# Two streams for the block inverses, and VectorE steps pinned to the written order

## The chip, the cores and the metric

The kernel runs on one core of a Trainium2 chip. The time is device microseconds of one execution; lower is better. The core has five engines that run side by side, each working through its own queue in order: TensorE (PE in the profile; PEld is its weight load), VectorE (DVE), ScalarE (ACT), GpSimd (POOL), and SyncE (SP), which issues the DMAs here. An engine waits for another one only where the program makes it wait on a semaphore.

## The reference

One layer of a streaming encoder, for 64 sample tokens and 512 prompt tokens in float32, so 576 rows of width 1024:

```
h   = RMSNorm(x);  p = h @ w_in                       # r, k, v, three low-rank inputs, u, v_gmlp, gate_A, gate_B
o_A = RWKV-7 over p:  S = S * w_t + (S a_t) b_t^T + v_t k_t^T;  y_t = S r_t      # per head, 16 heads of 64
o_B = u * (tril(W_s) LayerNorm(v_gmlp) + b)
m   = sigmoid(gate_A) * (o_A @ w_proj_a) + sigmoid(gate_B) * (o_B @ w_proj_b)
x   = x + RMSNorm(m @ w_o);  x = x + RMSNorm(SwiGLU(RMSNorm(x)))
```

The recurrence for S is what the change touches. The kernel does not run it token by token. It cuts the tokens in chunks of 64 (9 chunks: one of the sample group, eight of the prompt), and within a chunk the rank-one updates of 64 tokens become one product with the inverse of a unit triangular 64 x 64 matrix. Between chunks only a short chain is left: the state of a chunk times a 128 x 128 matrix, plus a constant part.

## The kernel before

**Products.** All large products split each float32 operand into a high part (`whi`, made on ScalarE) and a rest (`wlo`, made on GpSimd, line 305, two halves of 512 columns for each weight block), and run three matmuls for each one. Weights come in blocks of 512 KB (`raw`).

**Pairs.** The 16 heads are worked off as 8 pairs. For each pair p there are these streams, each a Python generator:

- `elementwise(p)`: decays and normalised vectors from the projected r, k, v; among the rest a scan on VectorE (`L`, line 670) and the four scalings `AR` and `BK` (lines 719 to 722); then the chunk matrices `AB` and `AK` (matmuls named `am`). It writes the 16 x 16 diagonal blocks of `AB` to DRAM (`d_inv`, eight DMAs, line 750). It signals "A" once the second lot of `am` matmuls (32 of them) is issued and "elem" at its end.
- `turns(p)`: transposes, signals "tb" and "values".
- `inverse(p)`: the inverse of each 64 x 64 triangle. First the substitution: the 80 diagonal blocks of 16 x 16 are read from DRAM with one block on a partition (`M`, line 855), and 15 steps on VectorE follow, each a product into `Xt` (line 863) and an addition into `X` (line 866). Then the result goes back through DRAM into `IV` (one DMA out, line 868, eight in, line 872), and two levels of merging follow: VectorE transposes `IV` to `IT` (`turn()`, line 875), small matmuls `m`, `m`, and again `turn()`, matmuls `mp`, `mu`. It signals "it".
- `batch(p)`: from `IT`, matmuls `d`, then `e` and `c`, which VectorE turns into the chain matrices `TD` and the `AR` half (lines 966 and 967); signals "d", "inv", and after matmuls `y` "wide".
- `chain(p)`: seven steps; each is a matmul `pc` (two in the first step) and a sum on VectorE, `dst = pc + C` (line 1005; the destination is `S`, or `So` for the two final states). The next `pc` reads that sum. Signals "chain".
- `finish(p)`: group norm and gate, stores o_A ("oa").

**The order of the work.** The order of TensorE is written by a planner, the class `Weave`. It holds a clock, `now`, that each matmul moves on by an estimate. A stream yields the wait until its next piece (a number out of the table `LAT`, in microseconds, or an event with a number to add), and `run` issues whichever stream is due, the first in the list of streams before the others. When none is due it issues a slice of a large product (`pj`, the projections; later `gv`): three or six matmuls. So the numbers in `LAT` are no waits of the chip; they say how much other work the planner puts between two pieces of a stream.

TensorE keeps that order exactly (`manual_schedule`). On the other engines, the DMA queue of SP among them, the framework re-sorts the instructions by its own estimate of when each is ready. `tc.keep_in_program_order(ins)` restrains that: the instruction stays behind the one that was traced just before it on its engine. Before the change only the first product of a substitution and some others, `turn()` among them, are pinned so; the later substitution steps and the chain's sums are free to be moved.

`inv_all()` runs the inverses of the eight pairs one after the other: `inverse(p)` starts when "A" of pair p is signalled and `inverse(p - 1)` has ended. The streams stand in the list as `chain_all(), fin_all(), batch_all(), inv_all(), turn_all(), elem_all(), ...`.

Of the kernel before, what the change touches and what calls it, by code (L numbers as in the profile page):

```python
# [8 lines left out]
ALU = mybir.AluOpType  # L9
# [11 lines left out]
NPAIR = NH // 2  # L21
# [16 lines left out]
LAT = {  # L38
# [4 lines left out]

# [1 line left out]
}  # L45
# [15 lines left out]
SB = 16  # L61
NU = 2 * (64 // SB) * 10
# [171 lines left out]
def layer(tc, I, O):  # L234
# [35 lines left out]
    clk = Weave()  # L270
# [577 lines left out]
        clk.signal("values", hp_)  # L848


    def inverse(E):

        hp_, AB, di = E["hp"], E["AB"], d_inv[E["hp"]]
        M = rp.tile([P, SB, SB], F32, tag="M", name="M")[0:NU]
        sp.dma_start(M.rearrange("u s t -> u (s t)"), di[0].rearrange("h b u s t -> (h b u) (s t)"))
        X = rp.tile([P, SB, SB], F32, tag="X", name="X")[0:NU]
# [3 lines left out]
        for s in range(0, SB - 1):  # L860
            w, r = SB - 1 - s, s + 1
            t3 = tmp[:, 0:r * w].rearrange("u (j t) -> u j t", t=w)
            ins = dve.tensor_tensor(t3, X[:, 0:r, s:s + 1].broadcast_to([NU, r, w]), M[:, s:s + 1, s + 1:SB].broadcast_to([NU, r, w]), ALU.mult)  # L863
            if s == 0:
                tc.keep_in_program_order(ins)
            dve.tensor_tensor(X[:, 0:r, s + 1:SB], X[:, 0:r, s + 1:SB], t3, ALU.add)  # L866
            yield LAT["X"]
        sp.dma_start(di[1].rearrange("h b u s t -> (h b u) (s t)"), X.rearrange("p i t -> p (i t)"))
        for h in range(2):
            for b in range(64 // SB):  # L870
                r0_ = 64 * h + SB * b
                sp.dma_start(IV[r0_:r0_ + SB, :, SB * b:SB * b + SB], di[1, h, b].rearrange("u s t -> s u t"))
# [119 lines left out]
    def chain(E):  # L992


        AR, C, S0, hp_ = (E[n] for n in ("AR", "C", "S0", "hp"))
        add = lambda c: C[:, PLACE[c][1], PLACE[c][0], :]
        state = lambda c: S0 if c == 0 else add(1) if c == 2 else S[:, c, :]
        for n, cs in enumerate([(2, 0)] + [(c,) for c in range(3, NCH)]):
            pc = ps1c("pc").rearrange("p (i v) -> p i v", v=HD)
            for i, c in enumerate(cs):  # L1000
                mmul(pc[:, i], TD[:, c, :], state(c), start=True, stop=True)
            for i, c in enumerate(cs):
                last = c in (0, NCH - 1)
                dst = rp.tile([P, HD], F32, tag="So", bufs=2, name="So") if last else S[:, c + 1, :]
                dve.tensor_tensor(dst, pc[:, i], add(c), ALU.add)  # L1005
                if last:
                    sp.dma_start((O["wkv_s"] if c == 0 else O["wkv_p"])[hp_], dst)
            yield LAT["S"]

        yield (("wide", hp_), LAT["y"])  # L1010
        Y = E["Y"]
        yield from clk.free(2)
        py = [ps1("py", 2.2)[:, 0:320].rearrange("p (j v) -> p j v", v=HD) for _ in range(2)]
        for c, j, half_ in PLACES2:
            for h, rows in enumerate(HR):
                mmul(py[h][HR[half_], j], AR[rows, 1, c * 64:(c + 1) * 64], state(c)[rows], start=True, stop=True, skip_group_check=True)
        for h in range(2):
            dve.tensor_tensor(Y[:, :, HR[h]], py[h], Y[:, :, HR[h]], ALU.add)
        clk.signal("chain", hp_)
# [45 lines left out]
    def elem_all():  # L1065
# [13 lines left out]
        for i in range(2):  # L1079
            sp.dma_start(R["ln"][i][0:64], I["rows"][i:i + 1, :].broadcast_to([64, D]))  # L1080

    def inv_all():
        for p_ in range(NPAIR):
            yield (("A", p_), 0.0)
            yield from inverse(EV[p_])

    def turn_all():
        for p_ in range(NPAIR):
            yield (("A", p_), 0.0)
            yield from turns(EV[p_])  # L1090

    def batch_all():
        for p_ in range(NPAIR):
            yield from batch(EV[p_])

    def chain_all():
        for p_ in range(NPAIR):
            yield (("inv", p_), LAT["ch0"])
            yield from chain(EV[p_])

    def fin_all():
        for p_ in range(NPAIR):
            yield (("chain", p_), 0.0)
            yield from finish(EV[p_])
# [408 lines left out]
    with tc.manual_schedule(engines={mybir.EngineType.PE}):  # L1513
        lora = {0: lora_w(lora_raw(0), pin=False)}
        for nm, b in (("k", BLK_K), ("r", BLK_R), ("v", BLK_V)):
            take = Shifted(b, nm, scale=True)
            EV[0][nm] = [take(h, raw0[nm][:, HS[h]]) for h in range(2)][1]
            clk.signal(nm, 0)
        clk.run(chain_all(), fin_all(), batch_all(), inv_all(), turn_all(), elem_all(), norm1(0), norm1(1), norm2(0), norm2(1), hidden(), oa_all(), ob_all(),
                ln_all(), norm3(0), norm3(1))  # L1520
    R["o"].close()
    R["d0"].close()
# [19 lines left out]
```

## Time and profile before

| | |
|---|---|
| time, median of 3 runs | 1225.54 us (1216.94 to 1228.83) |
| the profiled execution | 1224.4 us, its span from the first to the last instruction 1222.6 us |
| PE busy | 1179.4 us of the span, 96% |
| DVE, ACT, POOL busy | 524.0, 466.9, 612.7 us |
| mean granted TensorE clock | 0.994 |
| pairs, about | 85 to 575 us of the span, some 58 us a pair |

A line of the timeline gives start, duration, engine, source line, operation, written tile and read tiles, shapes, count, and in brackets the idle time of the engine before it with what ended it. A line of the waits gives the waiting engine and tile, the releaser, the total in us, how often, and the longest. Since nearly every matmul is recorded by one helper (line 286), tile names tell the products apart. A line of the stretches gives, for each engine, busy us and the number of instructions; after them stand the granted clock as a share of full speed, the DMA share and GB/s.

### The profile page before, as it was taken

The numbers are of one execution on the slowest core, as the hardware profiler recorded it, in microseconds if no ns is written. First come the engines' busy times: TensorE is split into PE (matmuls) and PEld (weight loads), VectorE is DVE, ScalarE is ACT, GpSimd is POOL, SyncE is SP. The second block draws the span as 40 slices with busy tenths as digits, with TensorE's granted clock in tenths as the row PEclk, the third lists the DMA queues.
The fourth block names the chain that finished last, engine by engine and source line by source line (L and its number), as shares of the span: only waits on it lengthen the run. The fifth ranks groups of instructions, "written<-read, shape, count | busy, mean of one in ns | idle before, by whom it ended". The sixth has DMA issues, their size and how long they took to land.

```text
span 1222.6 us, 29930 instructions
## 1 busy us (share of the span) xinstructions
PE 1179.4 (96%) x12926; PEld 1145.2 (94%) x12926; DVE 524.0 (43%) x1081; ACT 466.9 (38%) x889; POOL 612.7 (50%) x484
## 2 busy tenths in 40 slices
PE   7999999999999999999899999899999999999997
PEld 6999889899998999999899999899999999999996
DVE  5756365656555655432615331753333333300003
ACT  5555534453545453342512333533222222222220
POOL 6675353546363535233645453566555655634442
PEclk9999999999999999999999999899999999999999
DMA  5243223132322222332644542332222222242222
GB/s 186 78 109 106 82 51 95 48 94 49 97 66 78 76 80 82 91 101 82 216 142 127 186 124 69 99 107 80 87 87 78 79 86 87 82 156 83 80 77 78
DMA packets 68276, 118.05 MB, mean 97 GB/s; under 512 B 30832, under 2 KB 36208, under 8 KB 68144
## 3 DMA queue, kind: packets, MB, share of 16 engines
q1 hardware_dynamic: 68000, 116.06, 31.5%
q8 instruction: 101, 1.65, 0.6%
q14 instruction: 31, 0.25, 0.1%
q10 hardware_dynamic: 144, 0.08, 0.0%
HBM read 99.83 MB, written 16.28 MB: 95 GB/s over the span
## 4 chain that ended last, share of the span: by engine, by line
PE 75%; DVE 14%; ACT 3%; DMA 3%; issue 3%; POOL 2%; SPq 0%; DVEq 0%; ACTq 0%; POOLq 0%
PE fg L286 21%; PE po L286 15%; PE pj L286 15%; PE pb L286 4%; PE pa L286 3%; PE gv L286 3%; DVE Xt L863 2%; DVE X L866 2%; PE am L286 1%; PE z L286 1%; PE m L286 1%; POOL wlo L305 1%; PE pc L286 1%; PE wv L286 1%; PE d L286 1%
## 5 line engine op out<-in xcount | busy, mean ns | idle before, releaser
L305 POOL TENSOR_TENSOR wlo<-raw,whi 128x512 fp32r<-128x512 f32 (+1 forms) x288 | 398.3, 1406 | 352.1 <-ACT whi L302 326.5
L302 ACT ACTIVATE whi<-raw 128x1024 fp32r<-128x1024 f32 x144 | 149.9, 1045 | 281.7 <-PE fg L286 174.6
L1293 DVE TENSOR_TENSOR rs<-rs,nsq 128x288 f32<-128x288 f32 (+2 forms) x12 | 9.0, 754 | 106.0 <-ACT nsq L1292 106.0
L1361 DVE TENSOR_TENSOR ft<-ft,fg 128x288 f32<-128x288 f32 x40 | 16.4, 451 | 68.2 <-PE fg L286 66.7
L1355 DVE TENSOR_TENSOR fg<-fg,rs 128x288 f32<-128x288 f32 x40 | 16.4, 453 | 63.3 <-PE fg L286 63.2
L1358 DVE SCALAR_TENSOR_TENSOR ft<-ft,fg 128x576 f32<-128x576 f32 (+1 forms) x24 | 28.8, 1200 | 18.7 <-ACT ft L1357 18.7
L1359 POOL TENSOR_TENSOR ft<-ft,rs 128x576 f32<-128x576 f32 (+1 forms) x24 | 31.8, 1324 | 7.1 <-DVE ft L1358 7.1
L688 POOL TENSOR_TENSOR aq<-aq,k 128x576 f32<-128x576 f32 x8 | 11.4, 1421 | 34.4 <-PE pc L286 30.0
L286 PE MATMUL pc<-S,TD 128*128 128x64 f32 x112 | 20.2, 262 | 8.6 <-DVE So L1005 8.6
L863 DVE TENSOR_TENSOR Xt<-X,M 80x15 f32<-80x15 f32 (+7 forms) x120 | 25.8, 215 | 4.8 <-DMA M<-d_inv 1.2
L286 PE MATMUL pj<-h5h,whi 128*128 128x288 f32 x88 | 27.8, 316 | 0.0
L286 PE MATMUL pj<-h1h,whi 128*128 128x288 f32 x88 | 27.8, 316 | 0.0
L286 PE MATMUL pj<-h0h,whi 128*128 128x288 f32 x88 | 27.8, 315 | 0.0
L286 PE MATMUL pj<-h2h,whi 128*128 128x288 f32 x88 | 27.7, 315 | 0.0
L286 PE MATMUL pj<-h6h,whi 128*128 128x288 f32 x88 | 27.5, 312 | 0.0
L286 PE MATMUL pj<-h7h,whi 128*128 128x288 f32 x88 | 27.3, 310 | 0.0
L286 PE MATMUL pj<-h4h,whi 128*128 128x288 f32 x88 | 27.2, 309 | 0.0
L286 PEld LDWEIGHTS pc<-S,TD 128*128 128x128 f32 x112 | 17.4, 189 | 10.3 <-DVE So L1005 10.2
L866 DVE TENSOR_TENSOR X<-X,Xt 80x15 f32<-80x15 f32 (+7 forms) x120 | 25.2, 210 | 4.1
L1036 POOL TENSOR_TENSOR gm<-gm,mhalf 128x10 f32<-128x10 f32 x8 | 16.1, 2011 | 21.5 <-DVE gm L1035 21.5
L286 PE MATMUL pj<-h3h,whi 128*128 128x288 f32 x88 | 26.8, 305 | 0.0
L286 PE MATMUL pj<-h0h,wlo 128*128 128x288 f32 x88 | 26.3, 299 | 0.2 <-POOL wlo L305 0.2
(1200 smaller groups left out, 4238.3 us busy)
## 6 DMA issues: line engine op xcount, KB each, us to landing
raw<-in_w_in SPq DMA_DIRECT2D x50, 512.0 KB, 3.7
raw<-in_w_gate SPq DMA_DIRECT2D x22, 512.0 KB, 3.6
raw<-in_w_up SPq DMA_DIRECT2D x22, 512.0 KB, 3.6
raw<-in_w_down SPq DMA_DIRECT2D x16, 512.0 KB, 3.5
raw<-in_w_gv SPq DMA_DIRECT2D x8, 512.0 KB, 3.8
raw<-in_w_proj_a SPq DMA_DIRECT2D x8, 512.0 KB, 4.0
raw<-in_w_proj_b SPq DMA_DIRECT2D x8, 512.0 KB, 3.7
raw<-in_w_o SPq DMA_DIRECT2D x8, 512.0 KB, 3.6
```

Source lines behind the costliest of these rows:

```text
L286: return pe.matmul(out, lhsT, rhs, **kw)
L302: keep(act.activation(hi[:, :cols], raw[:, :cols], ACT.Copy))
L305: keep(pool.tensor_tensor(lo[:, c0:c1], raw[:, c0:c1], f(hi[:, c0:c1]), ALU.subtract))
L688: pool.tensor_tensor(aq, aq, k, ALU.mult)
L863: ins = dve.tensor_tensor(t3, X[:, 0:r, s:s + 1].broadcast_to([NU, r, w]), M[:, s:s + 1, s + 1:SB].broadcast_to([NU, r, w]), ALU.mult)
L866: dve.tensor_tensor(X[:, 0:r, s + 1:SB], X[:, 0:r, s + 1:SB], t3, ALU.add)
L1036: pool.tensor_tensor(m, m, mhalf, ALU.pow)
L1293: eng.tensor_tensor(acc[:, hs], acc[:, hs], q[:, hs], ALU.add)
L1355: keep(dve.tensor_tensor(g[:, HS[h]], pg, rs2[:, HS[h]], ALU.mult))
L1358: keep(dve.scalar_tensor_tensor(t[:, ts], t[:, ts], 1.0, g[:, ts], ALU.add, ALU.mult))
L1359: pool.tensor_tensor(t[:, ts], t[:, ts], rs2[:, ts], ALU.mult)
L1361: dve.tensor_tensor(t[:, HS[h]], t[:, HS[h]], pu, ALU.mult)
```

## The change

`inverse` is cut in two. The substitution, up to the DMA that writes `X` back, becomes a generator `substitute` with a stream of its own, `sub_all()`, which starts for pair p when "A" of p is signalled and the substitution of p - 1 has ended, and signals "x". What is left of `inverse` starts after "x", first waits a new number "O" (2.5), and then goes on as before. `sub_all()` stands behind `inv_all()` in the list of streams. Every product of the substitution is now pinned, not the first alone, and every sum of the chain is pinned. Two numbers are raised: "ch0" (between "inv" and the first chain step) from 6.0 to 7.5, and "S" (between chain steps) from 1.8 to 1.9. No instruction is added or taken out.

```diff
-    "M": 9.0, "X": 0.75, "U": 11.0, ...
-    "ch0": 6.0, "S": 1.8, "y": 0.5, ...
+    "M": 9.0, "X": 0.75, "O": 2.5, "U": 11.0, ...
+    "ch0": 7.5, "S": 1.9, "y": 0.5, ...
...
-    def inverse(E):
+    def substitute(E):
 
-        hp_, AB, di = E["hp"], E["AB"], d_inv[E["hp"]]
+        hp_, di = E["hp"], d_inv[E["hp"]]
...
         for s in range(0, SB - 1):
...
-            ins = dve.tensor_tensor(t3, X[:, 0:r, s:s + 1].broadcast_to([NU, r, w]), ..., ALU.mult)
-            if s == 0:
-                tc.keep_in_program_order(ins)
+            tc.keep_in_program_order(dve.tensor_tensor(t3, X[:, 0:r, s:s + 1].broadcast_to([NU, r, w]), ..., ALU.mult))
             dve.tensor_tensor(X[:, 0:r, s + 1:SB], X[:, 0:r, s + 1:SB], t3, ALU.add)
             yield LAT["X"]
         sp.dma_start(di[1].rearrange("h b u s t -> (h b u) (s t)"), X.rearrange("p i t -> p (i t)"))
+        clk.signal("x", hp_)
+
+    def inverse(E):
+
+        hp_, AB, di = E["hp"], E["AB"], d_inv[E["hp"]]
+        yield LAT["O"]
         for h in range(2):
...
-                dve.tensor_tensor(dst, pc[:, i], add(c), ALU.add)
+                tc.keep_in_program_order(dve.tensor_tensor(dst, pc[:, i], add(c), ALU.add))
...
+    def sub_all():
+        for p_ in range(NPAIR):
+            yield (("A", p_), 0.0)
+            yield from substitute(EV[p_])
+
     def inv_all():
         for p_ in range(NPAIR):
-            yield (("A", p_), 0.0)
+            yield (("x", p_), 0.0)
             yield from inverse(EV[p_])
...
-        clk.run(chain_all(), fin_all(), batch_all(), inv_all(), turn_all(), ...
+        clk.run(chain_all(), fin_all(), batch_all(), inv_all(), sub_all(), turn_all(), ...
```

More of the change, by code (lines that the diff above doesn't have):

```diff
@@ L862, in inverse @@
             t3 = tmp[:, 0:r * w].rearrange("u (j t) -> u j t", t=w)
-            ins = dve.tensor_tensor(t3, X[:, 0:r, s:s + 1].broadcast_to([NU, r, w]), M[:, s:s + 1, s + 1:SB].broadcast_to([NU, r, w]), ALU.mult)
-            if s == 0:
-                tc.keep_in_program_order(ins)
+            tc.keep_in_program_order(dve.tensor_tensor(t3, X[:, 0:r, s:s + 1].broadcast_to([NU, r, w]), M[:, s:s + 1, s + 1:SB].broadcast_to([NU, r, w]), ALU.mult))
             dve.tensor_tensor(X[:, 0:r, s + 1:SB], X[:, 0:r, s + 1:SB], t3, ALU.add)
@@ L1518, in layer @@
             clk.signal(nm, 0)
-        clk.run(chain_all(), fin_all(), batch_all(), inv_all(), turn_all(), elem_all(), norm1(0), norm1(1), norm2(0), norm2(1), hidden(), oa_all(), ob_all(),
+        clk.run(chain_all(), fin_all(), batch_all(), inv_all(), sub_all(), turn_all(), elem_all(), norm1(0), norm1(1), norm2(0), norm2(1), hidden(), oa_all(), ob_all(),
                 ln_all(), norm3(0), norm3(1))
```

4 rows, old and new, of the table LAT are left out of this document.

## The prediction

> **What bounds the kernel now.** I read first the page's engine rows, then the busy time by stretches, then who makes TensorE wait, and last the timelines around the longest of those waits.
>
> ```profile
> PE 1179.4 (96%) x12926; PEld 1145.2 (94%) x12926; DVE 524.0 (43%) x1081; ACT 466.9 (38%) x889; POOL 612.7 (50%) x484
> ```
>
> ```profile
> 85.00:530.00 445.00, 429.40 (x6941) 405.96 (x6931) 246.56 (x635) 210.71 (x477) 209.58 (x168) 1.00 0.28 80
> 530.00:575.00 45.00, 45.00 (x691) 43.52 (x691) 9.38 (x24) 16.73 (x36) 13.51 (x11) 1.00 0.21 65
> 575.00:630.00 55.00, 51.30 (x437) 49.88 (x436) 23.84 (x50) 21.28 (x31) 26.86 (x22) 1.00 0.56 179
> ```
>
> TensorE is the bound. The first figure behind the length of a stretch is its busy time: while the pairs run (85 to 530 us) it is idle for 445.0 - 429.4 = 15.6 us, in the next stretch for nothing, and from 575 to 630 us for 3.7 us. The change leaves the number of matmuls as it is, so all it can win is these 19.3 us, 1.6% of the time; what it can lose has no such bound. The waits of TensorE say whose they are:
>
> ```profile
> PE pc L286 <- DVE So L1005: 8.6, 7, 1.8
> PE m L286 <- DVE IT L875: 1.8, 3, 0.9
> PE pa L286 <- ACT s L448: 1.7, 1, 1.7
> PE gv L286 <- POOL wlo L305: 1.7, 2, 1.4
> PE m L286 <- ACT whi L302: 1.6, 1, 1.6
> PE m L286 <- ACT gq L1032: 0.7, 1, 0.7
> PE pj L286 <- POOL wlo L305: 0.2, 1, 0.2
> ```
>
> The chain's matmuls wait 8.6 us for the chain's sums, seven times, over half of the 15.6 us. The merging matmuls `m` wait 1.8 + 1.6 + 0.7 = 4.1 us. The projections wait 0.2 us for weights: those are loaded far enough ahead. VectorE's timeline at one of the seven places shows why the sum is late:
>
> ```profile
> 384.32 0.22 DVE L967 TENSOR_TENSOR AR<-c,AR 128x64 f32<-128x64 f32 x1
> 384.46 0.16 DVE L863 TENSOR_TENSOR Xt<-X,M 80x15 f32<-80x15 f32 x1
> ...
> 391.64 0.18 DVE L866 TENSOR_TENSOR X<-X,Xt 80x15 f32<-80x15 f32 x1
> 391.74 0.21 DVE L1005 TENSOR_TENSOR S<-pc,C 128x64 f32<-128x64 f32 x1
> 391.87 0.21 DVE L1005 TENSOR_TENSOR So<-pc,C 128x64 f32<-128x64 f32 x1
> ```
>
> ```profile
> 359.00 1.10 PE L286 MATMUL am<-AR,BK 64*64 64x128 f32 x32
> 369.91 0.82 PE L286 MATMUL mu<-PT,IV 32*32 32x32 f32 x40
> 388.63 0.39 PE L286 MATMUL pc<-S,TD 128*128 128x64 f32 x2
> 392.13 0.43 PE L286 MATMUL pc<-S,TD 128*128 128x64 f32 x2 [1.07 <-DVE So L1005]
> ```
>
> The 15 substitution steps stand as one block of 391.82 - 384.46 = 7.4 us between the `TD` and `AR` work of `batch` and the chain's first sums. The first `pc` is done at 389.0, its sum comes at 391.74, and the second `pc` waits 1.07 us for it. The last pair has no substitution behind it, and its stretch (530 to 575 us) has no idle time at all. So the block is the cause, not the length of the chain.
>
> **The change part by part.**
>
> *The substitution as its own stream.* Before, it starts behind `mu` of the pair before (369.91 + 0.82 = 370.7); now behind "A", the end of `am` x32 (360.1). That is 10.6 us earlier in the order, with the same wait "M" of 9.0 for the same `M`; its first step then is due at about 384.5 - 10.6 = 374, and 15 waits of 0.75 take it to 385 at least, longer by what other work stands between. It so runs in a part of VectorE's time that is half empty:
>
> ```profile
> 366.71 0.76 DVE L1049 TENSOR_TENSOR oo<-oo,bonus 128x576 f32<-128x576 f32 x1 [2.19 <-ACT oo L1047]
> 372.81 0.46 DVE L790 TENSOR_TENSOR bonus<-bo,v 128x288 f32<-128x288 f32 x1 [3.54 <-PE bo L286]
> 375.60 0.46 DVE L790 TENSOR_TENSOR bonus<-bo,v 128x288 f32<-128x288 f32 x1 [2.33 <-PE bo L286]
> 379.46 2.08 DVE L670 TENSOR_TENSOR_SCAN L<-rmask,sg 128x576 f32<-128x576 f32 x1 [3.41 <-ACT sg L668]
> ```
>
> The brackets hold 11.5 us of idle time for 7.4 us of steps. The merging follows 10.6 - 2.5 ("O") = 8.1 us earlier than now, and the chain, behind the longer "ch0", 8.1 - 1.5 = 6.6 us earlier; seven steps each 0.1 longer leave 5.9 us at its end. A chain that starts at 382 thus still shares a few microseconds with the end of the next substitution, but with steps that lie apart and in order, so that a sum has one or two of them ahead of it and not thirty. The sums' wait of 8.6 us I take as gone: -8.6, bounds 0 (the block only moves along) and -8.6.
>
> *What moves with it.* The substitution brings the load of `X`, the store of `X` and, in `inverse`, eight loads of `IV`, all in SP's queue:
>
> ```profile
> 308.48 0.31 SPq L855 DMA_DIRECT2D M<-d_inv  x1
> 333.45 0.34 SPq L868 DMA_DIRECT2D d_inv<-X  x1
> 335.19 4.67 SPq L872 DMA_DIRECT2D IV<-d_inv  x8
> ```
>
> `M` is issued right after its source already, so it hardly moves. The store and the eight loads (0.34 + 4.67 us of issue) move some 8 us ahead, past one or two weight blocks. Those have the cover of the 0.2 us row above: I put this at nothing; with that cover gone, each pair's next block would come up to 5 us late.
>
> *The pins.* What is queued behind a waiting pinned sum is VectorE's whole later work, and for the sum it is the `pc` after it. How much a chain step can bear is in these rows:
>
> ```profile
> 336.16 0.33 PE L286 MATMUL pc<-S,TD 128*128 128x64 f32 x2
> 336.53 0.22 DVE L1005 TENSOR_TENSOR S<-pc,C 128x64 f32<-128x64 f32 x1 [2.10 <-PE pc L286]
> 338.46 0.33 PE L286 MATMUL pc<-S,TD 128*128 128x64 f32 x2
> ```
>
> A step needs 336.53 - 336.16 = 0.37 us to the sum, 0.22 us for it, and some 0.06 us to the next `pc` (So ended at 392.08, `pc` began at 392.13): 0.65 of the 2.30 us between two steps. So 1.65 us are free. What can hold VectorE longer is a step that itself is held, and the trace has that once:
>
> ```profile
> 501.97 1.18 DVE L866 TENSOR_TENSOR X<-X,Xt 80x63 f32<-80x63 f32 x1
> 503.19 1.21 DVE L863 TENSOR_TENSOR Xt<-X,M 80x64 f32<-80x64 f32 x1
> 504.43 0.22 DVE L866 TENSOR_TENSOR X<-X,Xt 80x64 f32<-80x64 f32 x1
> ```
>
> ```profile
> 501.72 2.60 POOL L305 TENSOR_TENSOR wlo<-raw,whi 128x512 fp32r<-128x512 f32 x2 [8.70 <-ACT whi L302]
> ```
>
> While GpSimd makes the two halves of a weight rest, two steps take 1.2 us each and not 0.22; they end as the halves end. Today the block mostly lies where GpSimd is idle; spread out it won't. A chain sum behind both comes 1.18 + 1.21 = 2.39 us late, a stall of 2.39 - 1.65 = 0.74 us. How often:
>
> ```profile
> L305 POOL TENSOR_TENSOR wlo<-raw,whi 128x512 fp32r<-128x512 f32 x82 | 113.1, 1401 | 92.7 <-ACT whi L302 76.3 <-issue 13.1 <-PE tb L290 3.3
> ```
>
> These halves take 113.1 of the 445 us, a quarter, so of the seven chains that overlap a substitution about two meet a pair of them: 2 x 0.74 = +1.5 us; bounds 0, and 10.4 if all seven meet it twice.
>
> [...]
>
> *The end of the pairs.* The wait of `pa` for ScalarE's split of the last o_A (1.7 us) hangs on the last chain by way of its `finish`; with that chain 5.9 us earlier it goes: -1.7, bounds 0 and -1.7. Next late would be `gv` with its 1.7 us for weights, which the change doesn't touch: nothing.
>
> *The merging.* `turn()` stays pinned, and `m` keeps its 2.3 us behind it. Its 4.1 us of waits come from what ScalarE and VectorE happen to be doing, and that is shuffled: I take no change, bounds -4.1 and +4.1. One of these waits has a price beside it:
>
> ```profile
> 175.00:180.00 5.00, 3.42 (x100) 3.18 (x98) 4.96 (x7) 1.81 (x5) 1.29 (x1) 0.95 0.39 105
> 180.00:185.00 5.00, 5.00 (x63) 4.55 (x64) 2.52 (x4) 0.78 (x2) 3.37 (x3) 0.71 0.01 3
> ```
>
> After a stretch with 1.6 us of idle time the granted clock is 0.95 and then 0.71, which is 5 x (0.05 + 0.29) = 1.7 us of lost work. If that wait goes, this can go too; the sum leaves it out.
>
> **The sum.** -8.6 + 1.5 - 1.7 = -8.8 us. Against the profiled execution's own 1224.4 us that gives 1215.6; its time is 1.1 us under the median of 1225.5, and against the median it gives 1216.7. I predict 1217, or 0.7% less; with the terms' bounds mixed, 1211 to 1222 for this case. About 1% (12.3 us) is the least that can be told from no change here, the three runs of before being 11.9 us apart.
>
> **The rivals.**
>
> *All of it goes.* The chain's 8.6, the merging's 4.1, `pa`'s and `gv`'s 1.7 each and the clock's 1.7 us sum to 17.8: 1207.7. For it: an earlier substitution gives the merging room. Against it: the merging's waits are for three different releasers, and two of them are on ScalarE, whose other work the change leaves where it is. Chance 0.20.
>
> [...] All seven overlapping chains meet the two held steps twice: -8.6 - 1.7 + 10.4 = +0.1, 1225.6. Against it: 113.1 of 445 us is a quarter and not all. Chance 0.17.
>
> *The block only moves along.* `batch` comes earlier too (by 8.1 us), so that the pinned steps pile up behind its `TD` work and the chain meets them as before; only `pa`'s 1.7 us go: 1223.8. Against it: 15 waits stand between the steps in the order, and all are kept now. Chance 0.08.
>
> *Slower: `turn()` stands in VectorE's queue.* It needs `IV`. From the store of `X`, which follows the block's end at once (333.45), the trace takes until 339.86 (the end of the eight issues) and then the landing:
>
> ```profile
> DMA to landing us min/median/max: 1.6/1.8/3.8
> ```
>
> That is 8.2 us; the order gives 2.5 + 11.0 = 13.5, so the substitution may end 5.3 us later on the chip than in the order. Pinned behind `TD`, `AR` and the scan and held by GpSimd, it could lag more; then the pinned `turn()` waits at the head of VectorE's queue, the chain's sums behind it, and `m` and `pc` on TensorE. It decides from a lag of 5.3 us on; at 8 us each of the eight pairs loses 2.7, together 21.6: 1225.5 - 10.3 + 21.6 = 1236.8. Against it: the steps use 7.4 of the 11.25 us or more that they are given, and two held ones add 2.0. Chance 0.10.
>
> The forecast keeps 0.45. **Numbers:** the range of 1206 to 1231 holds the forecast and three rivals, and the mild half of the fourth; beyond it lie the strong half and ends that I didn't think of. Faster by over 1% (under 1213.3): the first rival and 0.06 from the forecast's low end, 0.26. Slower by over 1% (over 1237.8): half of the last rival and a little for the unforeseen, 0.08. Within 1%: 0.66.
>
> **What would show it.** Right: no row for `pc` waiting on `So`, or one under 2 us; `Xt` steps in groups of one or two between other work, from 10 us before the `TD` work on; `d` some 8 us nearer to `am` x32; no wait of `pa` for ScalarE. [...] Wrong: a `pc` wait as long as before, a `turn()` whose idle time ends with a load of `IV`, `pj` waiting for `wlo` or `whi`, or a new wait of TensorE over 9 us in the waits.

## The result and the profile after

The changed kernel takes 1235.26 us (median of 10 runs, 1225.87 to 1237.8); the kernel before, run beside it, 1220.79 us (10 runs, 1216.94 to 1228.83). The ratio is 1.0082 with a 95% interval of 1.0056 to 1.0108: some 0.8%, or 10 us, slower. The two medians lie further apart, 14.5 us, because the ten times of the kernel before fall into two groups, 1216.9 to 1220.8 and 1225.5 to 1228.8 us, and its median lies in the lower one. The forecast was 1217 us.

The profiled execution of the changed kernel took 1225.87 us, the shortest of its ten; its span is 1224.1 us at a mean granted clock of 0.989. A second trace of the same program, from the run called e1 below, has 1233.3 us at 0.984 and stands for it better, so both are read here ("The clock" below says where the 9 us between them lie).

The engine row of the page and the stretches of the changed kernel, columns as before:

```profile
PE 1176.7 (96%) x12926; PEld 1142.6 (93%) x12926; DVE 552.2 (45%) x1081; ACT 466.5 (38%) x889; POOL 615.0 (50%) x484
```

```profile
85.00:530.00 445.00, 424.63 (x6829) 401.56 (x6832) 273.09 (x634) 207.70 (x473) 205.96 (x164) 0.99 0.28 78
530.00:575.00 45.00, 45.00 (x746) 43.35 (x746) 10.39 (x25) 16.53 (x35) 14.54 (x11) 0.96 0.27 81
575.00:630.00 55.00, 52.03 (x451) 50.59 (x450) 23.19 (x45) 22.58 (x34) 27.76 (x21) 1.00 0.50 163
```

While the pairs run, TensorE is idle for 445.0 - 424.6 = 20.4 us, where it was 15.6. VectorE, with the same 1081 instructions, is busy for 552.2 instead of 524.0 us. Whose the waits are (waits of TensorE, changed kernel):

```profile
PE pc L286 <- DVE S L1009: 5.3, 4, 2.1
PE m L286 <- DVE IT L879: 4.0, 2, 3.1
PE mp L286 <- DVE Xt L863: 3.2, 1, 3.2
PE mp L286 <- DVE AB L743: 2.8, 1, 2.8
...
PE pa L286 <- ACT s L448: 1.4, 1, 1.4
PE gv L286 <- POOL wlo L305: 1.4, 3, 0.8
...
PE m L286 <- ACT gq L1036: 1.2, 1, 1.2
...
PE m L286 <- DVE AB L743: 1.0, 1, 1.0
PE mp L286 <- DVE IT L879: 0.7, 1, 0.7
```

The chain's waits fell from 8.6 to 5.3 us and did not go. The waits of the merging (`m` and `mp`) rose from 4.1 to 4.0 + 3.2 + 2.8 + 1.2 + 1.0 + 0.7 = 12.9 us (11.6 us in the second trace). So 3.3 us are won and 8.8 lost.

**The order that the planner makes of it.** The timeline of TensorE shows the merging matmul `mp` against the next pair's `am` x32, after which "A" is signalled. First the kernel before, then the changed one:

```profile
242.63 1.40 PE L286 MATMUL am<-AR,BK 64*64 64x128 f32 x32
250.60 0.82 PE L286 MATMUL mp<-IT,AB 32*32 32x32 f32 x40
...
301.38 1.10 PE L286 MATMUL am<-AR,BK 64*64 64x128 f32 x32
309.10 0.82 PE L286 MATMUL mp<-IT,AB 32*32 32x32 f32 x40
```

```profile
240.46 1.10 PE L286 MATMUL am<-AR,BK 64*64 64x128 f32 x32
251.17 0.82 PE L286 MATMUL mp<-IT,AB 32*32 32x32 f32 x40 [3.17 <-DVE Xt L863]
...
304.54 0.82 PE L286 MATMUL mp<-IT,AB 32*32 32x32 f32 x40 [2.83 <-DVE AB L743]
305.88 1.10 PE L286 MATMUL am<-AR,BK 64*64 64x128 f32 x32
...
338.49 0.43 PE L286 MATMUL pc<-S,TD 128*128 128x64 f32 x2 [2.06 <-DVE S L1009]
```

In these pairs of the kernel before, `mp` comes 7.7 to 8.0 us behind that `am`. Now it comes in turn 10.7 us behind it and 1.3 us ahead of it. The prediction had it 8.1 us earlier everywhere. The whole pattern of a pair follows suit; here are three neighbouring pairs of each trace, all in us behind the start of `am` x32 (the kernel e13 is told of below):

| | `mp` | substitution, first to last step | chain's first `pc` |
|---|---|---|---|
| before | 8.0, 7.7, 8.0 | 25.7-33.1, 24.7-32.0, 25.5-32.8 | 29.0, 28.5, 29.5 |
| after | 10.7, -1.3, 10.1 | 9.0-33.2, 14.1-32.8, 8.0-31.0 | 34.9, 20.5, 32.4 |
| e13 | 15.5, -1.3, 15.5 | 13.3-29.4, 14.2-33.5, 13.3-29.4 | 36.7, 20.6, 36.7 |

The substitution does begin 11 to 18 us earlier, but it ends where it ended before: spread out, it lasts 19 to 24 us in these pairs instead of 7. In one kind of pair (call it late) the chain now follows it, and there no `pc` waits. In the other kind (early) the chain begins some 12 us before the substitution ends, and each of the four `pc` waits of the row above lies in an early pair (at 217, 221, 338 and 450 us). The two kinds take turns over the whole run, less evenly at its ends: in the last late pair `mp` comes 4.5 us behind that `am`.

**What stands ahead in VectorE's queue.** Two `pc`, at 217 and 221 us, wait 1.4 us each for a sum that stands behind substitution steps held by GpSimd, as the prediction's part on the pins describes; ahead of the first of them:

```profile
215.65 1.40 DVE L864 TENSOR_TENSOR X<-X,Xt 80x39 f32<-80x39 f32 x1
216.98 0.21 DVE L1009 TENSOR_TENSOR S<-pc,C 128x64 f32<-128x64 f32 x1
```

GpSimd's instruction on line 688 ran from 215.60 to 217.00 us beside the step, which ended at 217.05; the same step takes 0.20 us at 334.75 us.

VectorE's timeline ahead of the `pc` at 338.49 us, the longest of the four waits, shows another reason:

```profile
337.48 0.52 DVE L489 SCALAR_TENSOR_TENSOR k<-pj,omm,q 128x288 f32<-128x288 f32 x1 [2.54 <-ACT q L487]
337.91 0.17 DVE L863 TENSOR_TENSOR Xt<-X,M 80x28 f32<-80x28 f32 x1
338.12 0.18 DVE L864 TENSOR_TENSOR X<-X,Xt 80x28 f32<-80x28 f32 x1
338.22 0.21 DVE L1009 TENSOR_TENSOR S<-pc,C 128x64 f32<-128x64 f32 x1
```

The pinned sum, and the pinned step ahead of it, stand behind `k`, which waits 2.54 us for ScalarE. Ahead of the `mp` at 251.17 us (a late pair):

```profile
242.07 1.28 DVE L760 TENSOR_TENSOR AK<-am,cst 128x512 f32<-128x512 f32 x2
249.46 0.17 DVE L863 TENSOR_TENSOR Xt<-X,M 80x15 f32<-80x15 f32 x1 [6.11 <-DMA M<-d_inv]
...
250.19 0.83 DVE L879 STREAM_TRANSPOSE IT<-IV 128x640 f32<-128x640 f32 x1
```

The next pair's first substitution step, pinned before and after, waits 6.11 us for its load `M`, and the second `turn()` of the merging, on which `mp` hangs, stands behind it. (Of the two `turn()` in the program only the first is pinned, before and after; the second was free to be moved and still landed here.) Before, that step came behind `mu` in the order and so met no `turn()`. The page's row of the groups has the sum of such waits at its end; the same row before had 1.2 us, once:

```profile
L863 DVE TENSOR_TENSOR Xt<-X,M 80x15 f32<-80x15 f32 (+7 forms) x120 | 37.9, 315 | 18.8 <-DMA M<-d_inv 16.2
```

And ahead of the `mp` at 304.54 us (an early pair):

```profile
302.10 1.78 DVE L1042 TENSOR_TENSOR Y<-Y,gm 128x640 f32<-128x640 f32 x1 [2.07 <-POOL gm L1040]
303.80 1.28 DVE L743 TENSOR_TENSOR AB<-am,rmul 128x512 f32<-128x512 f32 x2
```

Here `mp` waits for the product that empties the first of `am`'s accumulators (line 743); the small products share a ring of accumulators, so I read this as a wait for a free one. That product stands behind the group norm of the pair before, which waits 2.07 us for GpSimd. In the kernel before, line 743 ran 4.9 us ahead of that product of the group norm there (298.25 and 303.19 us). One long wait is of a plainer kind: at 472.61 us `m` waits 3.14 us for a `turn()` that stands at the end of some 10 us of unbroken work on VectorE, scalings and group norm among it, none of which waits for anything.

**The clock.** Idle time alone does not make 10 us. Of 85 to 640 us, TensorE was idle for 19.3 us before, 23.5 after and 22.6 in the second trace. But the granted clock fell. The same wait of 2.83 us, the same program, two executions: stretches of the first trace, and then of the second.

```profile
304.00:308.00 4.00, 3.46 (x108) 2.92 (x110) 3.26 (x9) 1.66 (x4) 3.11 (x3) 1.00 0.08 9
308.00:312.00 4.00, 4.00 (x74) 3.80 (x67) 0.33 (x1) 0.89 (x3) 1.05 (x3) 1.00 0.33 33
```

```profile
245.00:250.00 5.00, 2.62 (x49) 2.35 (x49) 2.81 (x10) 1.63 (x3) 0.00 (x0) 0.82 0.17 63
250.00:255.00 5.00, 5.00 (x56) 4.66 (x56) 0.91 (x2) 1.02 (x4) 2.92 (x3) 0.50 0.30 98
255.00:260.00 5.00, 5.00 (x51) 4.84 (x52) 0.79 (x3) 1.14 (x3) 0.00 (x0) 0.65 0.33 108
...
304.00:308.00 4.00, 3.50 (x77) 2.97 (x78) 2.74 (x8) 1.27 (x3) 2.60 (x3) 0.78 0.09 11
308.00:312.00 4.00, 4.00 (x53) 3.66 (x52) 0.82 (x2) 1.27 (x3) 1.52 (x3) 0.50 0.41 44
```

In the second trace the clock is granted at half after the wait, and TensorE gets through 53 matmuls in the 4 us in which the first trace has 74; the rows from 245 us on show the same after a wait of 2.38 us. What one such drop costs can be read by itself. From `am` x32 at 305.88 us (second trace: 305.84) to the next pair's `am` x48 at 353.69 us (356.64), both executions run the same 647 matmuls with the same idle time (2.06 and 2.05 us), at a mean granted clock of 1.00 and 0.93; they take 47.81 and 50.80 us, so the drop costs 3.0 us.

The end of the program has to be kept apart. From the first `po` matmul on (722.37 us before, 730.45 and 732.39 in the two traces after) the kernels run the same 3630 matmuls in the same order, but this rest takes 500.2 us before and 493.6 and 501.0 us after. One stretch of it, in the first and then in the second trace:

```profile
860.00:1060.00 200.00, 200.00 (x1541) 200.00 (x1540) 66.69 (x96) 56.03 (x65) 120.08 (x81) 1.00 0.28 85
```

```profile
860.00:1060.00 200.00, 200.00 (x1502) 200.00 (x1501) 64.87 (x93) 53.95 (x62) 116.78 (x78) 1.00 0.28 83
```

TensorE is never idle in it and the granted clock is 1.00, and still one execution gets through 1541 matmuls and the other through 1502, as many as the kernel before. No run here shows why. It makes the first trace some 7 us shorter by luck, and it may be what parts the two groups of the kernel before, which is not shown.

So the change's own cost is what has come together up to the first `po`: 8.1 us in the first trace and 10.0 us in the second. Of this, 4.2 and 3.8 us are idle time of TensorE (30.0 us before, 34.2 and 33.7 after), and 3.9 and 6.3 us are longer busy time. What the clock can have cost I estimate as (1 - clock) x span, which in the stretch from `am` x32 on gives 0.07 x 50.80 = 3.6 us where 3.0 were measured: 7.3 us before, 13.5 and 19.7 us after. That is 6.2 and 12.4 us more, enough for the longer busy time in both.

### The profile page after: what moved, and what is told of

The parts are those of the page before. It is cut to its first block, busy times and chain, and to the rows that moved or that the text cites. A ratio compares the mean times of both kernels' runs of the same rounds, so it can differ in the third digit from the quotient of the medians.

```text
span 1224.1 us, 29924 instructions
## 1 busy us (share of the span) xinstructions
PE 1176.7 (96%) x12926; PEld 1142.6 (93%) x12926; DVE 552.2 (45%) x1081; ACT 466.5 (38%) x889; POOL 615.0 (50%) x484
## 4 chain that ended last, share of the span: by engine, by line
PE 80%; DVE 10%; ACT 3%; issue 2%; DMA 2%; POOL 2%; SPq 1%; DVEq 0%; POOLq 0%; ACTq 0%
PE fg L286 20%; PE pj L286 17%; PE po L286 15%; PE pb L286 4%; PE gv L286 3%; PE pa L286 3%; PE z L286 2%; PE am L286 1%; PE fp L286 1%; PE y L286 1%; PE d L286 1%; PE c L286 1%; PE pc L286 1%; POOL wlo L305 1%; DVE y L1336 1%
## 5 line engine op out<-in xcount | busy, mean ns | idle before, releaser
L863 DVE TENSOR_TENSOR Xt<-X,M 80x15 f32<-80x15 f32 (+7 forms) x120 | 37.9, 315 | 18.8 <-DMA M<-d_inv 16.2
L864 DVE TENSOR_TENSOR X<-X,Xt 80x15 f32<-80x15 f32 (+7 forms) x120 | 38.6, 322 | 4.1
L1009 DVE TENSOR_TENSOR S<-pc,C 128x64 f32<-128x64 f32 x48 | 10.3, 216 | 41.9 <-PE pc L286 35.1
L702 POOL TENSOR_TENSOR rmul<-cst,rn 128x1280 f32<-128x1280 f32 x8 | 19.0, 2378 | 16.5 <-DVE S L1009 8.8
L286 PE MATMUL pj<-h2h,wlo 128*128 128x288 f32 x88 | 26.5, 301 | 0.0
```

The lines of the kernel that those rows point to most:

```text
L286: return pe.matmul(out, lhsT, rhs, **kw)
L702: pool.tensor_tensor(rmul.rearrange("p j h t -> p (j h) t"), mask.unsqueeze(1).broadcast_to([P, 10, P]), rn.unsqueeze(2).broadcast_to([P, ...
L863: tc.keep_in_program_order(dve.tensor_tensor(t3, X[:, 0:r, s:s + 1].broadcast_to([NU, r, w]), M[:, s:s + 1, s + 1:SB].broadcast_to([NU, r, ...
```

## The experiments

**e1: the changed kernel again.**

> The changed kernel once more, nothing edited, for a second trace and a clock beside the others. Theory A (the first substitution step, pinned, waits for M at the head of VectorE's queue, turn() stands behind it, and TensorE's waits for IT of about 3 us then lower its clock): again 1230 to 1238 us, a wait of Xt for M of 10 to 25 us in sum, m and mp waiting 6 us or more, granted clock under 0.99. Theory B (held steps make the pinned chain sums late): pc waits of 5 us or more, and those would go with the longer times.

1234.09 us (4 runs), the kernel before beside it 1225.32; ratio 1.0075 (1.0056 to 1.0094). The loss is real. The waits of the chain and of the merging are those above to 0.1 us, but for the `mp` behind `M` with 2.4 instead of 3.2 and the `mp` behind `IT` with 0.2 instead of 0.7; both theories' signs are there.

**e2: a longer wait for `M` in the order.** The first theory (A): the loss is the wait of the pinned first step for `M`.

> Edit: the number M (from A to the first substitution step in the order) 13.0 and not 9.0; pair 0 keeps its 7.0. Theory A: the wait of Xt for M falls from 16.2 us to under 3, the waits of mp and m that come from it (some 7 us) go, the granted clock comes back to 0.99 or more, and the time falls by 7 to 14 us against the changed kernel. Theory B: the steps come 4 us later and nearer to the chain, so the pc waits stay at 5 us or grow, and the time stays within 4 us of the changed kernel.

```diff
-    "M": 9.0,
+    "M": 13.0,
```

1240.42 us, ratio 1.014 (1.0112 to 1.0168): slower still. The wait for `M` fell from 16.2 to 0.8 us, but the substitution now ends 4 to 9 us later behind its `am` and so meets more of the chain (waits of TensorE, e2; two waits of `pc` for `So` add 2.2 us):

```profile
PE pc L286 <- DVE S L1009: 12.9, 5, 4.4
...
PE m L286 <- ACT gq L1036: 3.9, 1, 3.9
```

Theory A missed; but this kernel has another order as well, so it does not settle it.

**e3 and e4: the split alone, the pins alone.**

> Edit: the two streams and O stay, but chain sums and all substitution steps after the first are free again, and ch0 and S have their old numbers. Theory A: the first step is still pinned and still early, so the wait for M and the time over the kernel before stay, within 4 us of the changed kernel. Theory B (the pins are the harm): about as fast as the kernel before or faster, 1212 to 1222 us, pc waits under 4 us.

```diff
 # the changed kernel, with
-    "ch0": 7.5, "S": 1.9
+    "ch0": 6.0, "S": 1.8
 # and only the first step pinned, the sums free
```

> Edit: the kernel before with all substitution steps and the chain sums pinned, one stream, old numbers. Theory A: no wait for M at the head of the queue (under 3 us), the clock as in the kernel before, the time within 6 us of it. Theory B: pc waits of 9 us or more, some behind steps of 1.2 us, and 6 to 15 us slower than the kernel before.

```diff
 # the kernel before, with every product of the substitution and every sum pinned
+            tc.keep_in_program_order(dve.tensor_tensor(t3, ...))
+                tc.keep_in_program_order(dve.tensor_tensor(dst, pc[:, i], add(c), ALU.add))
```

The split alone: 1254.66 us, ratio 1.0241 (1.0215 to 1.0267). The pins alone: 1237.8 us, 1.0104 (1.0089 to 1.0119). Each part costs by itself, the split far more than both together and the pins about as much. Neither theory had a time near 1254 for e3; e4 came out as theory B expected. In e3, with later steps free, `to` waits 10.8 us for line 760, and the steps wait 27.4 us for `M`. In e4 TensorE's order is that of before, matmul by matmul, so its trace shows what the pins do to the other engines. Waits of TensorE, VectorE's timeline and GpSimd's:

```profile
PE pc L286 <- DVE S L1003: 16.7, 13, 3.3
```

```profile
396.11 1.50 DVE L864 TENSOR_TENSOR X<-X,Xt 80x63 f32<-80x63 f32 x1
397.64 1.20 DVE L863 TENSOR_TENSOR Xt<-X,M 80x64 f32<-80x64 f32 x1
398.87 1.18 DVE L864 TENSOR_TENSOR X<-X,Xt 80x64 f32<-80x64 f32 x1
399.98 0.21 DVE L1003 TENSOR_TENSOR S<-pc,C 128x64 f32<-128x64 f32 x1
```

```profile
396.09 1.44 POOL L688 TENSOR_TENSOR aq<-aq,k 128x576 f32<-128x576 f32 x1 [8.42 <-PE pc L286]
397.47 2.50 POOL L305 TENSOR_TENSOR wlo<-raw,whi 128x512 fp32r<-128x512 f32 x2
```

Three steps of 1.2 to 1.5 us instead of 0.2 end as GpSimd's instructions end, and the sum stands behind them. Of the 240 instructions of the substitution, those over 0.6 us are 3 before, 28 after and 35 in e4; what they take above 0.21 us sums to 2.5, 27.3 and 35.2 us.

**e5: a substitution that does not wait for the pair's `M`.** `M` is loaded from constants instead of the pair's blocks, so that the substitution solves nothing; all instructions stay.

> Edit of the changed kernel: M is loaded from a constant input (unit blocks) and not from the blocks that AB was written to, so the substitution solves nothing and the inverses are left out of the result; every instruction but that DMA's source stays, and the order on TensorE is the same. Theory A (the wait for M at the head of VectorE's queue is what the split costs): the wait of Xt for M is under 1 us, mp and m no longer wait 2 to 3 us, the granted clock is 0.99 or more, and the time falls by 8 us or more against the changed kernel, to 1226 or less. Rival C (the split costs because the substitution is spread and held by GpSimd): the wait for M goes, but the time stays within 4 us of the changed kernel.

```diff
-        sp.dma_start(M.rearrange("u s t -> u (s t)"), di[0].rearrange("h b u s t -> (h b u) (s t)"))
+        sp.dma_start(M.rearrange("u s t -> u (s t)"), I["cst"][0:NU, C_X0:NCST])
```

1233.17 us (10 runs), ratio 1.0066 (1.0041 to 1.0092): as slow as the changed kernel. No step waits for `M`, and the `mp` behind it is free; `am` now waits 2.9 us for a step once and `m` for line 743 2.3 instead of 1.0 us, the first with a wait of VectorE for the constants' load of `X` (3.4 us, once). TensorE's order is that of the changed kernel, but VectorE's is not quite: with nothing of the pair to wait for, some first steps run 16 to 25 us earlier (168.05 us instead of 192.69), so the edit takes away more than a wait. Even so, a kernel without the wait is as slow: it is one of several that take each other's place, and not by itself the cause. Theory A falls.

**e6 and e7: the longer set waits alone, on the kernel before.**

> Edit of the kernel before: only the numbers ch0 (7.5) and S (1.9) of the change, no split, no pins. If the block of steps ahead of the chain is what made pc wait 8.6 us, 1.5 us more before the chain takes 7 x 1.1 us or so of it away: pc waits of 1 to 3 us, time 4 to 8 us under the kernel before. If the chain's sums would be late anyway, pc waits of 7 us or more and the same time.

> Edit of the kernel before: ch0 8.5, S stays 1.8, no split, no pins. By the same reasoning no pc wait over 0.5 us is left, and the time is 6 to 10 us under the kernel before; a candidate for the fastest version. By the rival pc waits elsewhere in the chain and the time stays.

```diff
 # e6
-    "ch0": 6.0, "S": 1.8
+    "ch0": 7.5, "S": 1.9
 # e7
-    "ch0": 6.0
+    "ch0": 8.5
```

1239.31 us, ratio 1.0114 (1.0076 to 1.0151), and 1252.9 us, 1.0236 (1.0196 to 1.0275). In e6 the `pc` waits are 12.2 us; in e7 `m` waits 12.2 us for ScalarE. Both were expected to be faster, by 4 to 8 and by 6 to 10 us. Moving the chain by 1.5 us (with 0.1 us more for each step) or by 2.5 us in the old order costs 14 and 27 us. Both moves have a price, and the prediction set the price of its own at nothing; that the order before had been fitted to its numbers is my reading of this.

**e8, e9 and e10: GpSimd reading less.** The rest `wlo` of a weight is set to zero by an instruction that only writes and reads nothing, so the low part of the weights is left out of the products. e8 is e4 with that, e9 the kernel before, e10 the changed kernel. The theory (D): pins cost because GpSimd's reads hold the steps ahead of a sum. Beside it (C'): the split costs by itself.

> Edit of the pins-only kernel (the kernel before with all substitution steps and the chain sums pinned): the rests wlo are set to zero by a GpSimd instruction that reads nothing, so the low part of the weights is left out of the result; count and order of the matmuls stay. Theory D (a step with two inputs in SBUF is held by a GpSimd instruction that reads SBUF, and pinned sums behind it come late): nearly all steps of 1.2 us go, the pc waits fall from 16.7 us to 8 or less, and the time falls by 6 us or more against pins only. Rival E (the sums are late because of what else is queued ahead of them): pc waits stay at 12 us or more.

> Edit of the kernel before: the rests wlo are set to zero by a GpSimd instruction that reads nothing (the low part of the weights is left out of the result), as in the pins-only kernel with the same edit (1201.1 us). It is the base for what pins and split cost without most of GpSimd's reads. Theory D (the pins cost because spread steps are held by GpSimd's reads): this base is no faster than pins only with the edit, 1199 to 1205 us, and its pc waits stay near 8 us since the block still stands ahead of the chain. Rival E (the pins cost by their order alone): this base is 8 to 14 us faster than that kernel, 1187 to 1193 us.

> Edit of the changed kernel: the same zero rests. Theory D: with the reads gone the split and the pins do what was forecast, 3 to 9 us faster than the kernel before with the same edit, m and mp waits under 4 us, clock 0.995 or more. Rival C' (the new order on VectorE costs whatever GpSimd does): as much slower than that base as the change was, 6 to 12 us.

```diff
-            keep(pool.tensor_tensor(lo[:, c0:c1], raw[:, c0:c1], f(hi[:, c0:c1]), ALU.subtract))
+            keep(pool.memset(f(lo[:, c0:c1]), 0.0))
```

The three take 1201.06, 1202.42 and 1214.75 us, with ratios to the kernel before of 0.9806 (0.9771 to 0.9842), 0.9831 (0.9791 to 0.9872) and 0.9933 (0.9902 to 0.9963). With GpSimd's reads, pins cost 12.5 us (e4, 1237.8 against 1225.3); without them, nothing that can be told (1201.1 against 1202.4), and the waits of TensorE show why (e8, to be held beside the 16.7 us of e4):

```profile
PE pc L286 <- DVE S L1003: 3.4, 6, 1.2
```

(In e8 18 instructions of the substitution are still over 0.6 us, where theory D expected nearly all to go; GpSimd's other instructions read as before.) TensorE's order is the same in the kernel before, e4, e8 and e9. So theory D holds for the pins, in the main: when GpSimd no longer reads to make `wlo`, the cost of the pins goes. (The instruction that only writes is shorter too: two take 0.99 us at 332.36 us in e8, where the reading ones took 2.60 us at 501.72 us before. Which of the two it is, the reading or the length, these runs do not part.) But the changed kernel is still 1214.75 - 1202.42 = 12.3 us over the kernel before with only 3 held instructions left, where theory D expected it 3 to 9 us under it and C' 6 to 12 us over it: what the split and the set waits cost does not come from held steps. C' holds beside it. (The zeros also make the kernel before 23 us shorter; how much of that is GpSimd's reads and how much the shorter way from a load to its products, these runs do not part.)

**e11 and e12: the changed kernel with one kind of pin taken back.**

> Edit of the changed kernel: the chain's sums are not pinned, all else stays. Split only costs 29 us and the whole change 9; this tells which pins take the difference away. If the pins of the steps do it: within 4 us of the changed kernel. If the pins of the sums do it: 1245 us or more.

> Edit of the changed kernel: only the first product of a substitution is pinned, as before the change; the sums' pins, the split and the numbers stay. If the pins of the steps are what holds the split's harm down: 1245 us or more, with the steps in blocks of fifteen behind a wait for M and long waits of TensorE for what stands behind the block. If not: within 4 us of the changed kernel.

```diff
 # e11
-                tc.keep_in_program_order(dve.tensor_tensor(dst, pc[:, i], add(c), ALU.add))
+                dve.tensor_tensor(dst, pc[:, i], add(c), ALU.add)
 # e12: only the first product of a substitution is pinned, as before
```

Without the pins of the sums 1225.4 us (10 runs), ratio 1.0026 (0.9999 to 1.0053); the `pc` waits fall from 5.3 to 1.2 us. TensorE's order is that of the changed kernel, and the time can no longer be told from the kernel before, though the merging still waits as long. Without those of the steps 1242.04 us, 1.0141 (1.0078 to 1.0203); `y`, `c` and `mp` wait on VectorE for 5.3, 3.2 and 4.8 us. Neither run fell where its expectation had put it (within 4 us of the changed kernel, or at 1245 us or more). The pins of the sums cost about 0.5%, some 6 us, more than the 4 us of waits that they bring. The split seems to need the pins of the steps, but the interval of e12 overlaps that of the changed kernel, so this is likely and not shown.

**e13, e14 and e15: the merging later.** The theory (F): the merging stands in the wrong place, and 8.1 us more in "O" take back the move worked out in the prediction.

> Edit of the changed kernel: O is 10.6 and not 2.5, so the merging stands about where it stood before the change, while the substitution stays early. Theory F: the waits of m and mp fall from 11.9 us to 5 or less, the clock rises to 0.988 or more, and the time falls by 5 us or more, to 1229 or less; the pinned sums still cost some pc waits. Rival C' (any new order on VectorE costs): the waits move elsewhere, time within 4 us of the changed kernel or longer.

> Edit: O 10.6 and the chain's sums not pinned. Theory F: both costs gone, so 5 us or more under the kernel with free sums alone (1225.4): 1220 or less, faster than the kernel before, clock 0.990 or more. Rival C': 1225 us or more.

> Edit: O 10.6, the chain's sums not pinned, and the old ch0 (6.0) and S (1.8). The longer numbers alone made the kernel before 14 us slower; theory F says that this came from the same kind of collision, so with them undone the order is nearest to that of before with the substitution taken out of the chain's way: 1212 to 1220 us. Rival C': 1225 us or more.

```diff
 # e13
-    "O": 2.5
+    "O": 10.6
 # e14: also the sums not pinned; e15: also "ch0": 6.0, "S": 1.8
```

e13 takes 1212.41 us (1211.61 to 1215.19), the kernel before beside it 1224.08; ratio 0.9908 (0.9886 to 0.993). It is the best version found, 0.9% faster than before and 1.7% faster than the changed kernel by the ratios. e14: 1212.28 us, 0.9895 (0.9877 to 0.9913), the same. e15: 1240.49 us, 1.013 (1.011 to 1.015). TensorE's waits and its timeline in e13:

```profile
PE pc L286 <- DVE S L1009: 2.6, 4, 0.8
...
PE mp L286 <- DVE AB L743: 1.8, 3, 0.8
```

```profile
239.80 1.10 PE L286 MATMUL am<-AR,BK 64*64 64x128 f32 x32
255.30 0.82 PE L286 MATMUL mp<-IT,AB 32*32 32x32 f32 x40
...
301.51 0.82 PE L286 MATMUL mp<-IT,AB 32*32 32x32 f32 x40 [0.75 <-DVE AB L743]
302.85 1.10 PE L286 MATMUL am<-AR,BK 64*64 64x128 f32 x32
```

The merging's waits shrink to 0.8 us or less, and no `turn()` stands behind an `M`: the steps wait 1.3 us for it in all. Still 26 instructions of the substitution are held, 24 us in sum; in the late pairs they lie ahead of the chain and nobody waits for them, and in the early ones no `pc` waits over 0.8 us. But the mechanism expected is not what the trace shows. The merging did not go back to its old place: it alternates as in the changed kernel, with 15.5 us in the late pairs (10.7 there) and -1.3 in the early ones. The early pairs kept their place in the order. There `mp` waits 0.3 to 0.8 us in each, where in the changed kernel one of them waited 2.83 us and the others not at all; at that one it is 0.75 us now, because the group norm ahead of line 743 comes some 2 us sooner behind their `am` (line 1042 starts 3.0 us behind the start of `am` x48, and 5.0 us in the second trace of the changed kernel). In sum TensorE is idle for 9.7 us from 85 to 640 us instead of 22.6, and (1 - clock) x span is 10.9 us instead of 19.7.

e15 shows what the longer set waits are for: with the old ones the chain comes 1.5 us earlier into the substitution, and `pc` waits 9.0 us, eight times. Theory F had 1212 to 1220 us for it and missed.

**e16 and e17: other values of "O".**

> Edit of the changed kernel: O is 6.0, between 2.5 (1234 to 1235 us) and 10.6 (1212 us). Theory F: the merging still reaches into VectorE's full part, so the time lies between, 1217 to 1233 us, with m and mp waits between 4 and 12 us. One lucky value: 1230 us or more, with waits elsewhere.

> Edit of the changed kernel: O is 13.0. Theory F: the merging still lies behind VectorE's full part, m and mp waits 5 us or less, and the chain comes 2.4 us later than with 10.6, which TensorE's other work covers: 1209 to 1220 us. One lucky value: 1225 us or more.

```diff
 # e16
-    "O": 2.5
+    "O": 6.0
 # e17
+    "O": 13.0
```

1254.6 us, ratio 1.0239 (1.0224 to 1.0254), and 1242.51 us, 1.0139 (1.0105 to 1.0172). So 2.5, 6.0, 10.6 and 13.0 give ratios of 1.008, 1.024, 0.991 and 1.014. Both runs missed what theory F expected of them and came out as its rival said, that 10.6 is one lucky value. At 6.0 the first steps wait 28.7 us for `M` and `mp` 6.4 us behind them, `m` 8.6 us for ScalarE; at 13.0 `pc` waits 10.9 us. It is not a curve with a best place but a new order each time, with collisions of its own. That the first value tried is the good one is luck; why 10.6 has so few collisions, beyond where its waits are gone, stays open, and another value may be better yet.

## Why the prediction was wrong

**The sums' waits, -8.6.** Measured -3.3, with the held steps' part in it. The prediction took the substitution's start (10.6 us earlier) and added 15 waits of 0.75 us for its end; that the start moves, the table above bears out. The end did not: the steps stand among other planned work and last 19 to 24 us. So the relief came in the late pairs alone, by the chain moving back, and in the early ones the chain moved 8 us forward into the substitution. The note "longer by what other work stands between" was the place to stop and work this out.

**The held steps, +1.5, bounds 0 and 10.4.** That GpSimd holds steps was right, and e4 with e8 shows it at work: pins cost 12.5 us while GpSimd makes `wlo` and nothing that can be told when it only writes zeros; a held step stands ahead of a pinned sum. Its size was too small: in the changed kernel the two waits at 217 and 221 us alone are 2.8 us. The steps now lie where GpSimd works, and 28 of 240 are held where 3 were; the estimate of two of seven chains took GpSimd's share of the time for the share of steps that it meets. Of the changed kernel's own loss the pins of the sums are some 0.5% (e11), not all of it by held steps: the longest `pc` wait stands behind `k`, which waits for ScalarE. The opening sentences say that an engine waits for another one only where the program makes it wait on a semaphore; these traces show otherwise, as in the step of 1.40 us at 215.65 us, on VectorE, which needs nothing that GpSimd's instruction beside it makes.

**The merging, "I take no change", bounds -4.1 and +4.1.** This is the step that failed, together with the end of the substitution above. Measured +8.8 (7.5 in the second trace), about twice the bound. Its ground was that the merging would only be shuffled against ScalarE and VectorE. In fact two things were new: the order alternates between two places of the merging, which no uniform shift of 8.1 us gives; and a second stream puts instructions with waits of their own, a pinned one among them, ahead of `turn()`. Neither is in a row of the trace of before, but the second could be asked of the change: of each instruction that is pinned ahead of a moved one, what does *it* wait for. The prediction asked that of the sums and of `turn()`, not of the first step. It also took both `turn()` for pinned, where only the first is.

**The clock, "the sum leaves it out".** The row was there (1.6 us of waiting, then 0.95 and 0.71), and it was read only as a gain that might come. Priced on the loss side it is about half of the result in the first trace and more in the second: 3.9 and 6.3 us of longer busy time, beside single waits of 2.4 to 3.2 us in the merging.

**`pa`, -1.7.** Measured -0.3: the last chain does not come earlier (its first `pc` at 561.2 us, before 559.0).

**The store and the loads, nothing.** Right: `gv` waits 1.4 us for weights (2.1 in the second trace, 1.7 before), and no wait of TensorE leads to a load of `IV`.

**The rivals.** "`turn()` stands in VectorE's queue" came nearest, 1236.8 us at a chance of 0.10. Its place and its victim `m` are right, its releaser is not, so the near number is luck: `turn()` had its `IV` and stood behind a step that waited for `M`, or behind scalings and group norm. "The block only moves along" has its part in the early pairs. By what the prediction said would show it: `d` came 9 us nearer to `am` only in every other pair (5 us behind it instead of 14), and the row for `So` gave way to one for `S` of 5.3 us. Steps of 1.2 to 1.4 us stand ahead of sums.

## What to carry to other kernels

Where a planner writes the order, a shift of one stream is not a shift: make the new order's pattern pair by pair first, and only then price the waits. Ask of each pinned instruction, also of those pinned already, what it waits for and who stands behind it on its engine. And price a new wait of the bound engine with the clock that it can cost (here 3.0 us behind a wait of 2.83 us, in one execution of two), not by its length alone.

## What the hardware showed beyond that

- In the second trace (e1) the wait of 2.38 us was followed by some 10 us at half clock and that of 2.83 us by some 7 us; these are estimates from the rows under "The clock", 2 x 5 x (0.18 + 0.50 + 0.35) = 10.3 us from 245 to 260 us, and 2 x 0.07 x 50.80 = 7.1 us from `am` x32 on. In the first trace none followed the same 2.83 us: 1.00 from 304 to 312 us. There, up to 640 us, the clock was granted at half four times, for 3.41 us each, from 252.06, 361.29, 473.93 and 531.96 us on; that is 109.23, 112.64 and 58.03 us after one another, or 32, 33 and 17 times 3.413 us. The wait of TensorE that ended last ahead of each was of 3.17, 1.02, 3.14 and 1.18 us, and had ended 0.9, 2.0, 1.3 and 2.0 us earlier. In the kernel before, a wait of 1.58 us ended at 178.96 us, and 3.41 us at half clock began at 179.48 us. So waits of 1.0 to 1.6 us were followed by a drop and one of 2.83 us was not; what decides it is not shown.
- In a stretch of 200 us (860 to 1060 us, changed kernel and e1) with TensorE never idle and the granted clock at 1.00, the same matmuls in the same order came to 1541 in one execution and 1502 in another. Two traces can so differ by some 7 us for a reason that neither idle time nor the clock shows; a part of the program that the change leaves alone is the place to look for it.
- In the trace of the changed kernel 28 substitution steps take 0.77 to 1.40 us instead of 0.2, and each ends 0.02 to 0.09 us behind the end of a GpSimd instruction (line 305, 688, 704 or 822); so do the three of the kernel before (0.75, 1.18 and 1.21 us). The chain's sums, which read `pc` from the matmuls' accumulators, took 0.20 to 0.23 us where they ran wholly inside such an instruction, 23 of 64 in the changed kernel, and at most 0.23 us before, 27 of 64. With zeros for `wlo` no step of the kernel before is over 0.22 us (e9).
